# Memory values of block two: computed within the attention and the router of block one instead of among the modulation's loads

## The chip, the cores and the metric

The kernel runs on one core of a Trainium2 chip. The metric is the device time of one execution in microseconds (us), the median of several runs. Engines are named as in the profile: PE is the matrix engine (PEld its weight loads), DVE, ACT and POOL the vector, scalar and general engines, SP the engine that issues most transfers.

## What is computed

Two blocks, one after the other, on 256 tokens of width 1024, all in 32-bit floats. Cut to what matters:

```python
# block one (x, ctx, c)
sh1, sc1, g1, sh2, sc2, g2 = split(silu(c) @ w_mod + b_mod, 6)     # modulation rows; the same for ctx
hx, hc = modulate(rmsnorm(x), sh1, sc1), modulate(rmsnorm(ctx), csh1, csc1)
...                                   # latents (w_in), MLA with 8 heads, neighbourhood attention with 8 heads
x = x + g1 * (concat([o_mla, o_na]) @ w_out)
hx2 = modulate(rmsnorm(x), sh2, sc2)
x = x + g2 * hierarchical_moe(hx2)    # 16 experts of 1024 x 512, router picks one group, two of its experts
# block two (the result of block one, and mem, 256 rows of width 1024)
kv = mem_n @ w_mem_kv                 # mem_n = rmsnorm(mem); 1024 x 2048
k, v = split(kv, 2)                   # "memory keys" and "memory values"
...                                   # w_in_2, convolution, stick-breaking attention
o = memory_cross_attention(q, rmsnorm(k), v)
...                                   # output projections, a feed-forward layer of 4096
```

Memory keys and values depend on `mem` and `w_mem_kv` alone. They may be computed at any time before block two's cross attention. The kernel computes both early and writes them to the scratch tensors `mkd` and `mvd` in device memory, from where block two reads them.

## The kernel before, in words

**Products.** A weight matrix comes in pieces of 128 x 4 x 512 floats (1024 KB, `raw` tiles). Each half of a piece (two groups of 128 rows) is made into a `split` tile: a rounded high part (ACT, L197, every fourth one DVE, L195) and the remainder (DVE, L198). PE then adds up three products: high times high, low times high, high times low (L223). A `Stream` S holds a list of such halves of all its jobs; `S.step()` does the next one, which with two halves of 128 tokens and 512 columns is 12 matmuls of 512 columns. `la[0]` says how many halves ahead the splits are made, `S.hold` where the list stops for now.

**Storage and loads.** The on-chip memory is cut into 24 slots. `take` takes the first of the free slots, `give` returns one. All weight loads stand in one list, `plan`, in a fixed order; `pump` issues the next ones on SP as slots come free (L138). SP works its queue in order: a load whose slot is still being read holds all loads behind it.

**Order of the work.** It is the order in which the program is written; each engine takes its instructions in that order.
1. Modulation (to 68.6 us): the memory keys (2 jobs, `J_mk`, `ev_memk`) and six of the eight steps of the memory values (`J_mv`, `ev_memv`, into the tile `mvt`) are put between the pieces of `w_mod`, whose products (`mod_rows`, L591) need 32 columns of weights only. `memTh`, `memTl` hold the transposed `mem_n`; `ktmp` the keys before their norm, `memk_T` transposes them.
2. `mod_T`: transposes and modulates `x` and `ctx` (ACT writes `md`, L662), and does one S step after each quarter: the last two steps of the values, then `kvl`. After the second quarter it gives `memTh`, `memTl`, and POOL's queue writes `mvt` to `mvd`.
3. Latents and projections of `w_in`; their last job is `nv`.
4. Attention: 32 units (16 neighbourhood units, then 16 MLA units) go through a pipeline of scores (PE L874, L877), maximum (DVE L886, L888), exponential (ACT L889), transposes of P (PE L483), and P times v (PE L912). The generator `latents()` interleaves, with the first half of the units, the MLA queries (`w_uq`) and keys and values (`w_ukv`; ACT L723 writes `kf`, DVE L724 writes `v`).
5. `w_out` (`J_wo`), residual, router (L995 to L1090), `gather` (L1113), which collects the tokens of an expert, then the 16 experts (L1186, L1215), whose weights stream in through `plan`.
6. Block two, whose weights follow in the same list.

Of the kernel before, what the change touches and what calls it, by code (L numbers as in the profile page):

```python
# [86 lines left out]
def body(tc, d, out, dbg=None, stop=None):  # L87
# [80 lines left out]
    class Stream:  # L168
# [62 lines left out]

        def step_w(self, job, s, k, kg, first, last):
# [117 lines left out]
    P_memv = [plan_w(("mv", c), d["w_mem_kv_2"], 1024, 1024 + 512 * c, 512) for c in range(2)]  # L350
    mvq = [plan.pop() for _ in range(4)][::-1]
    plan.append(mvq[0])
    plan_mod(0, range(2, 3))
    plan.append(mvq[1])
    plan_mod(0, range(3, 4))
    plan.append(mvq[2])
    plan_mod(0, range(4, 8))
    plan.append(mvq[3])
# [24 lines left out]
    P_ukv = [plan_w(("ukv", c), d["w_ukv"], 256, 512 * c, 512) for c in range(2)]  # L383
    P_wo = []
    for c in range(2):
        P_wo.append([(("wo", c, h), 4) for h in (1, 0)])
        for h in (1, 0):
            plan.append((("wo", c, h), [128, 4, 512], kpn(d["w_out"][512 * h:512 * h + 512, 512 * c:512 * c + 512])))
    for e in range(NE):
# [147 lines left out]
    mvt = take([128, 2, 1024], F32, "mvt")  # L537

    def ev_memv(c):
        def f(m, ps):  # L540
            A.activation(mvt[:, m, 512 * c:512 * c + 512], ps, AF.Identity, scale=rmem[:, m:m + 1])
# [36 lines left out]
    S.step()  # L578
    memk_T(0)
    sumsq(ss1[:, 0:1], x[:, 0, :])  # L580
    S.step()
    sumsq(ss1[:, 1:2], x[:, 1, :])
    S.step()
# [25 lines left out]
    S.step()  # L609
    next(mr)  # L610
    S.step()
    memk_T(1)
    give(ktmp)
    G.dma_start(mkd, mkT)
    dump("mkT", mkT)
    sumsq(ss1[:, 2:3], ctxt[:, 0, :])
    next(mr)
    S.step()
    sumsq(ss1[:, 3:4], ctxt[:, 1, :])
    S.step()  # L620
# [6 lines left out]
    la[0] = 1  # L627
    S.step()
    la[0] = 0
# [3 lines left out]
    S.ahead(1)  # L633
# [8 lines left out]
    S.ahead(2)  # L642
# [91 lines left out]
    for j in J_uq + J_ukv:  # L734
# [31 lines left out]
    give(mkT, mvt)  # L766
    st["ql"] = take([128, 2, 384], F32, "ql")
    interleave(S.gen(J_ql), (mod_rows(2, range(0, 4)), 1))

# [24 lines left out]
    S.hold = J_ukv[1].end  # L794
# [154 lines left out]
    for j in J_wo:  # L949
        S.add(j)  # L950
    side = latents()
    n = 0
    for i, _ in enumerate(pipeline(32, [at_s0, at_s1, at_s1b, at_s2, at_s3], [0, 0, 1, 3, 4])):
# [55 lines left out]

    S.run(J_wo[1])  # L1010
    give(oTh, oTl, gb[0])
# [28 lines left out]
    keep(1)  # L1040

# [81 lines left out]

    xg[0] = take([128, 8, 256], F32, "xg")
# [667 lines left out]
```

## Time and profile before

| | |
|---|---|
| Median of 3 runs (lowest, highest) | 1113.88 us (1113.6, 1114.24) |
| The profiled execution | 1112.18 us, of which the span of the trace is 1110.4 us |
| PE busy | 1057.2 us, 95% of the span |
| DVE, ACT, POOL busy | 606.0, 434.3, 93.3 us |
| Moved from and to device memory | 254.95 MB, mean 230 GB/s |
| The stages, us from the span's start | modulation to 68.6, latents to 176, attention to 272, `w_out` to 297, router and gather to 318, experts to 562, block two to the end |

A median compares kernels; a row of the trace belongs to the one profiled execution, so sums of rows are set against 1112.18. PE at 95% is a mean over stages: the rows below are cut by stage, since what an added matmul costs depends on whether PE waits there.

### The profile page before, as it was taken

Reading aid. Unit: us, or ns where it says so; the run is one execution under the profiler, and the core shown is the slowest. Engines: PE = TensorE matmul, PEld = TensorE weight load, DVE = VectorE, ACT = ScalarE, POOL = GpSimd, SP = SyncE. Lnnn points to the kernel's source line nnn. Section 1 sums busy time; section 2 is a strip of 40 time slices with the busy share of each in tenths; the row PEclk is TensorE's granted clock in tenths of the full one; section 3 lists DMA queues with packets and bytes.
Section 4 is the critical chain, followed back from the end, with each engine's and each line's share of the span. In section 5 each row is a group of like instructions: output and inputs, shape, how many; then the busy total and the mean of one; then the engine's idle time right before and its main releaser. Section 6 shows DMA issues by size and latency. Waiting matters only on the chain.

```text
span 1110.4 us, 15119 instructions
## 1 busy us (share of the span) xinstructions
PE 1057.2 (95%) x6115; PEld 789.3 (71%) x6115; DVE 606.0 (55%) x930; ACT 434.3 (39%) x744; POOL 93.3 (8%) x99
## 2 busy tenths in 40 slices
PE   5999999899989999998689999999999999999998
PEld 4678876555743434343279878999888889998997
DVE  4554435666534343433175655767455676666544
ACT  4754213556312222222163476444435125343222
POOL 0000303000101010100010444000000000000000
PEclk9999999999989999999899999999999999999999
DMA  9979852454868999999913342534757565545611
GB/s 337 405 259 400 278 181 73 176 190 162 326 230 315 393 395 392 394 395 394 387 61 115 114 153 76 190 124 155 258 184 251 204 207 172 190 154 189 225 41 38
DMA packets 111087, 254.95 MB, mean 230 GB/s; under 512 B 5434, under 2 KB 8475, under 8 KB 108451
## 3 DMA queue, kind: packets, MB, share of 16 engines
q1 hardware_dynamic: 109666, 249.20, 62.4%
q0 software_dynamic: 1344, 4.72, 1.4%
q8 instruction: 50, 0.82, 0.3%
q14 instruction: 27, 0.21, 0.1%
HBM read 249.71 MB, written 4.19 MB: 229 GB/s over the span
## 4 chain that ended last, share of the span: by engine, by line
PE 48%; DMA 1%; DVE 1%; ACT 1%; SPq 0%; issue 0%; DVEq 0%; ACTq 0%
PE acc L223 26%; PE acc L243 11%; PE b L243 7%; DMA raw<-in_w_in 1%; PE b L483 1%; PE b L1499 1%; PE b L1521 1%; PE b L1577 1%; PE b L1601 1%; PE b L1215 0%; PE b L1532 0%; SPq L138 0%; PE b L1520 0%; DVE split L198 0%; ACT junkB L476 0%
## 5 line engine op out<-in xcount | busy, mean ns | idle before, releaser
L198 DVE TENSOR_TENSOR split<-raw,split 128x1024 fp32r<-128x1024 f32 (+2 forms) x226 | 267.5, 1212 | 79.5 <-ACT split L197 77.4
L197 ACT ACTIVATE split<-raw 128x1024 fp32r<-128x1024 f32 (+2 forms) x170 | 168.2, 1035 | 42.4 <-PE acc L223 14.5
L243 PE MATMUL acc<-uh,split 128*128 128x256 f32 x640 | 122.9, 288 | 1.4 <-ACT uh L498 1.4
L1186 PE MATMUL b<-raw,xg 128*64 128x512 f32 x512 | 115.8, 595 | 0.0
L243 PEld LDWEIGHTS acc<-uh,split 128*128 128x128 f32 x640 | 102.7, 193 | 2.5 <-ACT uh L498 1.6
L223 PE MATMUL acc<-split,uh 128*128 128x512 f32 x320 | 101.2, 392 | 0.0
L243 PE MATMUL b<-fh,split 128*128 128x256 f32 x512 | 93.9, 283 | 0.3 <-DVE split L198 0.3
L243 PE MATMUL acc<-ul,split 128*128 128x256 f32 x320 | 91.4, 286 | 0.1
L223 PE MATMUL acc<-split,hidT 128*128 128x512 f32 x384 | 88.4, 389 | 0.0
L223 PEld LDWEIGHTS acc<-split,hidT 128*128 128x128 f32 x384 | 71.6, 188 | 14.6
L243 PEld LDWEIGHTS b<-fh,split 128*128 128x128 f32 x512 | 80.4, 192 | 0.8 <-DVE split L198 0.5
L1186 PEld LDWEIGHTS b<-raw,xg 128*64 128x64 f32 x512 | 36.5, 137 | 61.1 <-issue 59.0
L243 PE MATMUL b<-fl,split 128*128 128x256 f32 x256 | 72.4, 283 | 0.0
L223 PEld LDWEIGHTS acc<-split,uh 128*128 128x128 f32 x320 | 60.1, 188 | 12.8
L1225 ACT ACTIVATE RB<-RA 64x512 fp32r<-64x512 f32 x32 | 20.1, 628 | 121.8 <-DVE RA L1224 120.2
L1215 PE MATMUL b<-raw,RA 128*64 128x512 f32 x256 | 60.0, 611 | 5.3 <-ACT xg L1121 2.5
L243 PEld LDWEIGHTS acc<-ul,split 128*128 128x128 f32 x320 | 61.9, 193 | 0.7 <-DVE ul L499 0.6
L223 PE MATMUL acc<-split,ul 128*128 128x512 f32 x160 | 62.3, 390 | 0.0
L1224 DVE TENSOR_TENSOR RA<-b,gm 64x512 f32<-64x512 f32 x32 | 22.0, 689 | 71.9 <-PE b L1215 71.4
L243 PEld LDWEIGHTS b<-fl,split 128*128 128x128 f32 x256 | 49.1, 192 | 0.3
L1215 PEld LDWEIGHTS b<-raw,RA 128*64 128x64 f32 x256 | 19.0, 141 | 39.8 <-issue 34.4
L223 PE MATMUL acc<-split,memTh 128*128 128x512 f32 x128 | 44.0, 413 | 3.2 <-ACT split L197 1.7
(398 smaller groups left out, 1741.4 us busy)
## 6 DMA issues: line engine op xcount, KB each, us to landing
raw<-in_w_up SPq DMA_DIRECT2D x48, 1024.0 KB, 5.5
raw<-in_w_down SPq DMA_DIRECT2D x48, 1024.0 KB, 9.1
raw<-in_w_in SPq DMA_DIRECT2D x46, 1024.0 KB, 7.9
raw<-in_w_gate SPq DMA_DIRECT2D x32, 1024.0 KB, 14.8
raw<-in_w_mod SPq DMA_DIRECT2D x24, 1024.0 KB, 11.3
raw<-in_w_mem_kv SPq DMA_DIRECT2D x8, 1024.0 KB, 14.1
raw<-in_w_out SPq DMA_DIRECT2D x8, 1024.0 KB, 5.0
raw<-in_w_conv_out SPq DMA_DIRECT2D x4, 1024.0 KB, 4.9
```

The lines of the kernel that those rows point to most:

```text
L197: A.activation(s[:, 0], src, AF.Copy)
L198: V.tensor_tensor(s[:, 1], src, s[:, 0].bitcast(F32), op=OP.subtract)
L223: T.matmul(job.accs[m], x(k + kk), s[:, w, kk, :], start=job.start and first and kk == 0 and j == 0, stop=job.stop and last and kk == kg - ...
L243: T.matmul(bk[:, o:o + 256], s[:, w, kk, 128 * b:128 * b + 128], x(k + kk), start=first and b % per == 0 and r == 0 and kk == 0 and j == 0 ...
L483: T.transpose(bk[0:m, i * 128:i * 128 + p], s, ident)
L1186: T.matmul(b[64 * j:64 * j + 64, :], lt, raw((nm, e, k // 4))[:, k % 4, :], start=(k == 0), stop=(k == 7), skip_group_check=True)
L1215: T.matmul(b[64 * j:64 * j + 64, :], t[:, k, :], raw(("d", e, k // 2))[:, k % 2, 512 * dh:512 * dh + 512], start=(k == 0), stop=(k == 3), ...
L1224: V.tensor_tensor(RA[r, dh, :], b[r, :], gm[r, dh], op=OP.mult)
L1225: A.activation(RB[r, 0, dh, :], RA[r, dh, :], AF.Copy)
L1499: T.matmul(zb[i + j][:, o:o + 256 - k0], skT[sl, p, k0:k0 + 128], sqT[sl, p, k0:256], start=(o == 0), stop=False, skip_group_check=True)
L1521: T.matmul(b[:, 0:384], negL, v, start=False, stop=(n == 1), skip_group_check=True)
L1577: T.matmul(b[:, 0:256], xqT[:, 2 * h + dt, tt * 128:(tt + 1) * 128], mkT[:, 2 * h + dt, :], start=(dt == 0), stop=(dt == 1))
```

## The change

The loads of the memory values leave their places among the `w_mod` pieces. Those of the first job (columns 0 to 511, `J_mv[0]`) stand between `w_ukv` and `w_out`, those of the second behind `w_out`. The matmuls are issued by a new generator, `fine`, which does half a step at a time (6 matmuls of 512 columns, for one half of the tokens): the first job one half-step at every second unit from unit 15 on, that is in the MLA half of the attention; the second job four half-steps in the router, ahead of the matmuls that count the tokens of each expert, and four just ahead of `gather`. `mvt` is taken at unit 15, `memTh` and `memTl` are kept until `gather`, and the write to `mvd` is issued there. The steps that `mod_T` interleaves are then the last two of the memory keys, with their evacuation; `memk_T(1)` and the write of `mkd` move behind `kvl`. While `J_wo[1]` runs, `la[0]` is 4.

```diff
+        def fine(self, job):
+            while self.pos < job.end:
+                i = self.pos
+                while self.nprep <= i:
+                    self.prep(self.nprep)
+                    self.nprep += 1
...
+                for m, (hi, lo) in enumerate(job.lhs):
+                    for kk in range(kg):
+                        for j, (x, w) in enumerate(((hi, 0), (lo, 0), (hi, 1))):
+                            T.matmul(job.accs[m], x(k + kk), s[:, w, kk, :], start=first and kk == 0 and j == 0,
+                                     stop=last and kk == kg - 1 and j == 2)
+                    if last:
+                        job.evac(m, job.accs[m])
+                    if m == len(job.lhs) - 1:
+                        give(s)
+                        pump()
+                        self.pos += 1
+                        if self.nprep <= self.pos < job.end:
+                            self.prep(self.nprep)
+                            self.nprep += 1
+                    yield
...
     plan_mod(0, range(0, 2))
-    P_memv = [plan_w(("mv", c), d["w_mem_kv_2"], 1024, 1024 + 512 * c, 512) for c in range(2)]
-    mvq = [plan.pop() for _ in range(4)][::-1]
-    plan.append(mvq[0])
-    plan_mod(0, range(2, 3))
-    plan.append(mvq[1])
-    plan_mod(0, range(3, 4))
-    plan.append(mvq[2])
-    plan_mod(0, range(4, 8))
-    plan.append(mvq[3])
+    plan_mod(0, range(2, 8))
...
     P_ukv = [plan_w(("ukv", c), d["w_ukv"], 256, 512 * c, 512) for c in range(2)]
+    P_memv = [plan_w(("mv", 0), d["w_mem_kv_2"], 1024, 1024, 512)]
...
+    P_memv.append(plan_w(("mv", 1), d["w_mem_kv_2"], 1024, 1536, 512))
...
-    J_mv = [Job(P_memv[c], 512, mlhs, ev_memv(c)) for c in range(2)]
-    for j in J_mk + J_mv:
+    J_mv = [Job(P_memv[c], 512, mlhs, ev_memv(c), acc=(lambda: [bank(), bank()]) if c else None) for c in range(2)]
+    for j in J_mk:
         S.add(j)
...
     for i, _ in enumerate(mod_T()):
         S.step()
-        if i == 1:
-            give(memTh, memTl)
-            G.dma_start(mvd, mvt)
...
     S.run(J_kvl)
-    give(mkT, mvt)
+    memk_T(1)
+    give(ktmp)
+    G.dma_start(mkd, mkT)
...
-    for j in J_uq + J_ukv:
+    for j in J_uq + J_ukv + J_mv[:1]:
         S.add(j)
...
-    S.hold = J_ukv[1].end
+    S.hold = J_mv[0].end
...
-        elif side:
-            for _ in side:
+        elif mvg is None:
+            for _ in side or ():
                 pass
-            side = None
             lim[:] = [99, 3]
+            mvs["t"] = take([128, 2, 1024], F32, "mvt")
+            mvg = S.fine(J_mv[0])
+        if i >= 15 and i % 2:
+            next(mvg, None)
...
+    la[0] = 4
     S.run(J_wo[1])
+    la[0] = 2
...
     start_y(0, 1)
     keep(1)
+    mvg = S.fine(J_mv[1])
+    for _ in range(4):
+        next(mvg)
...
+    for _ in mvg:
+        pass
+    G.dma_start(mvd, mvs["t"])
+    give(memTh, memTl, mvs["t"])
     xg[0] = take([128, 8, 256], F32, "xg")
     for _ in gather(0):
         pass
```

Three places show what moves on the engines. Lines of the changed kernel have higher numbers: its split is still L197, the evacuations `P` and `kf` are L895 and L728, the matmuls of `fine` L246.

ACT at the start of the attention, before; `P` is the exponential of a unit, `q` and `kf` are evacuations of `w_uq` and `w_ukv` products, `raw_1597` is the second piece of `w_ukv`:

```order
L889 ACTIVATE P_160_1522,sm<-b_1528,sm 128x512
L197 ACTIVATE split_1580<-raw_1515 128x1024
L197 ACTIVATE split_1599<-raw_1597 128x1024
L714 ACTIVATE q_1534<-acc_1583,rq_r 128x384
L714 ACTIVATE q_1534<-acc_1584,rq_r 128x384
L889 ACTIVATE P_160_1522,sm<-b_1624,sm 128x512
L723 ACTIVATE kf_179_1634<-acc_1639,rkv_r 128x4x64
L723 ACTIVATE kf_179_1634<-acc_1640,rkv_r 128x4x64
```

The same place after the change; `raw_1459` is the second piece of `w_ukv`, `raw_1499` the first piece of the memory values:

```order
L895 ACTIVATE P_141_1380,sm<-b_1386,sm 128x512
L197 ACTIVATE split_1442<-raw_1440 128x1024
L197 ACTIVATE split_1461<-raw_1459 128x1024
L719 ACTIVATE q_1392<-acc_1445,rq_r 128x384
L719 ACTIVATE q_1392<-acc_1446,rq_r 128x384
L895 ACTIVATE P_141_1380,sm<-b_1484,sm 128x512
L197 ACTIVATE split_1501<-raw_1499 128x1024
L728 ACTIVATE kf_161_1494<-acc_1504,rkv_r 128x4x64
L728 ACTIVATE kf_161_1494<-acc_1505,rkv_r 128x4x64
```

The split of the first piece of the memory values now stands in ACT's queue between an exponential and the `kf` evacuations.

PE in the MLA half after the change (before, these rows are the same without the L246 ones, with L877 for L883 and L483 for L504); `kT`, `qT` are keys and queries of a pair of heads:

```order
L883 MATMUL b_1897<-kT_169_1551,qT_1617 128x512
L504 MATMUL b_1903<-cst,P_141_1380 128x128 x4
L246 MATMUL acc_1878<-split_1501,memTh_116 128x512
L246 MATMUL acc_1878<-split_1501,memTl_117 128x512
L246 MATMUL acc_1878<-split_1501,memTh_116 128x512 x2
L246 MATMUL acc_1878<-split_1501,memTl_117 128x512
L246 MATMUL acc_1878<-split_1501,memTh_116 128x512
L883 MATMUL b_1919<-kT_169_1551,qT_1617 128x512
L504 MATMUL b_1925<-cst,P_141_1380 128x128 x4
```

Six matmuls of 512 columns stand between every second pair of units.

PE in the router, before; L1008 starts a sum of the output, L1062 to L1064 count tokens, L1113 is `gather`:

```order
L1008 MATMUL acc_2538<-raw_84,cst 128x512
L1008 MATMUL acc_2551<-raw_84,cst 128x512
L1062 MATMUL b_2553<-selm,cst 128x32
L1063 MATMUL b_2553<-selm,ones 128x16
L1064 MATMUL b_2553<-selm,ones 128x32
L1113 MATMUL b_2581<-D_2560,xh_2527 128x256 x2
```

The same place after the change (L1079 to L1081 count tokens):

```order
L1020 MATMUL acc_2514<-raw_84,cst 128x512
L1079 MATMUL b_2516<-selm,cst 128x32
L1080 MATMUL b_2516<-selm,ones 128x16
L1081 MATMUL b_2516<-selm,ones 128x32
L246 MATMUL b_2473<-split_2380,memTh_116 128x512
L246 MATMUL b_2473<-split_2380,memTl_117 128x512
L246 MATMUL b_2473<-split_2380,memTh_116 128x512 x2
L246 MATMUL b_2473<-split_2380,memTl_117 128x512
L246 MATMUL b_2473<-split_2380,memTh_116 128x512
```

24 matmuls of the second job (from `split_2374` and `split_2377`) now stand ahead of the counting, and another 24 (from `split_2380` and `split_2395`) between the counting and `gather`.

## Rows read from the trace of the kernel before

**Rows 1.** Busy by stretch: length, PE, PEld, DVE, ACT, POOL, clock, DMA, GB/s

```profile
13.40:68.50 55.10, 52.64 (x256) 35.88 (x256) 30.07 (x62) 34.34 (x70) 0.72 (x1) 1.00 1.00 380
...
192.00:234.30 42.30, 36.11 (x214) 23.63 (x211) 27.25 (x66) 22.98 (x54) 0.79 (x4) 0.96 0.55 197
234.30:266.00 31.70, 31.70 (x162) 17.53 (x162) 21.66 (x52) 21.79 (x52) 0.00 (x0) 1.00 0.23 81
...
312.00:314.00 2.00, 2.00 (x11) 2.00 (x11) 0.59 (x5) 1.54 (x3) 0.00 (x0) 0.50 0.00 0
320.00:360.00 40.00, 38.06 (x186) 14.03 (x184) 16.43 (x24) 7.98 (x12) 4.86 (x2) 1.00 0.93 332
380.00:400.00 20.00, 20.00 (x101) 7.92 (x97) 5.71 (x10) 3.04 (x5) 0.00 (x0) 1.00 1.04 397
```

**Rows 2.** The chain that ended last: start, length (us), engine, what

```profile
548.22 13.97 DMA raw<-in_w_in
...
1084.42 21.80 PE acc L223 x96
```

**Rows 3.** Timeline of SP's DMA issues: start, length, what

```profile
18.63 0.91 SPq L138 DMA_DIRECT2D raw<-in_w_mod  x2
...
42.02 0.33 SPq L138 DMA_DIRECT2D raw<-in_w_mod  x1
```

**Rows 4.** DMA issues in 18.6:18.7, 42.0:42.1: KB of one, us to landing

```profile
raw<-in_w_mod SPq DMA_DIRECT2D x1, 1024.0 KB, 10.6
...
raw<-in_w_mod SPq DMA_DIRECT2D x1, 1024.0 KB, 12.7
```

**Rows 5.** Timeline of PE, end of the modulation: start, length, line, operation [idle before]

```profile
64.06 3.64 PE L591 MATMUL b<-raw,cond 128*32 128x512 f32 x32
68.57 1.09 PE L483 MATMUL b<-cst,raw 128*128 128x128 f32 x8 [0.87 <-DVE raw L597]
```

**Rows 6.** Timeline of ACT, memory-key and memory-value evacuations

```profile
28.32 0.67 ACT L518 ACTIVATE ktmp<-acc,rmem 128x512 f32<-128x512 f32 x1
...
32.20 0.21 ACT L468 ACTIVATE rk_r<-rk_t 128x4 f32<-128x4 f32 x1
...
75.73 1.50 ACT L541 ACTIVATE mvt<-acc,rmem 128x512 f32<-128x512 f32 x2
```

**Rows 7.** DMA issues in 163.0:163.42 and 182.2:182.6: KB, us to landing

```profile
raw<-in_w_ukv SPq DMA_DIRECT2D x1, 512.0 KB, 4.5
...
raw<-in_w_out SPq DMA_DIRECT2D x1, 1024.0 KB, 5.0
```

**Rows 8.** Timelines at the attention's start: PE, DVE, ACT

```profile
175.24 1.06 PE L591 MATMUL b<-raw,cond 128*32 128x512 f32 x8
...
181.58 0.57 DVE L198 TENSOR_TENSOR split<-raw,split 128x384 fp32r<-128x384 f32 x1
...
189.14 0.83 ACT L723 ACTIVATE kf<-acc,rkv_r 128x256 f32<-128x256 f32 x2
```

**Rows 9.** Timeline of PE, one period of the MLA units

```profile
242.19 1.12 PE L877 MATMUL b<-kT,qT 96*128 96x512 f32 x2
...
247.76 2.41 PE L912 MATMUL acc<-PT,v 128*64 128x256 f32 x16
250.10 1.13 PE L877 MATMUL b<-kT,qT 96*128 96x512 f32 x2
```

**Rows 10.** Timeline of DVE, end of w_out

```profile
295.60 0.69 DVE L941 TENSOR_TENSOR gb<-acc,gb 128x512 f32<-128x512 f32 x1 [5.61 <-PE acc L223]
```

**Rows 11.** Timeline of PE, router and gather

```profile
309.14 0.61 PE L1062 MATMUL b<-selm,cst 128*128 128x32 f32 x2 [4.79 <-DVE selm L1057]
...
311.70 2.05 PE L1113 MATMUL b<-D,xh 128*128 128x256 f32 x8 [1.10 <-DVE tot L1079]
...
318.26 8.80 PE L1186 MATMUL b<-raw,xg 128*64 128x512 f32 x40
```

**Rows 12.** DMA issues in 77.53:77.6: KB, us to landing

```profile
mvd<-mvt POOLq DMA_DIRECT2D x1, 1024.0 KB, 10.0
```

More of the change, by code (lines that the diff above doesn't have):

```diff
@@ L230, in step @@
             self.pos += 1
+        def fine(self, job):
[4 more added lines that the diff above has]
+                    self.nprep += 1
+                job, key, a, k, kg, first, last, done = self.g[i]
+                s = self.prepared.pop(i)
+                if first:
+                    job.accs = job.acc() if job.acc else [bank("acc")[:, :job.n] for _ in job.lhs]
+                for m, (hi, lo) in enumerate(job.lhs):
[13 more added lines that the diff above has]
+                    yield
         def step_w(self, job, s, k, kg, first, last):
@@ L536, in body @@
     mlhs = lhs_of(memTh, memTl, (0, 128))
-    mvt = take([128, 2, 1024], F32, "mvt")
+    mvs = {}
     def ev_memv(c):
         def f(m, ps):
-            A.activation(mvt[:, m, 512 * c:512 * c + 512], ps, AF.Identity, scale=rmem[:, m:m + 1])
+            A.activation(mvs["t"][:, m, 512 * c:512 * c + 512], ps, AF.Identity, scale=rmem[:, m:m + 1])
         return f
     J_mk = [Job(P_memk[c], 512, mlhs, ev_memk(c)) for c in range(2)]
-    J_mv = [Job(P_memv[c], 512, mlhs, ev_memv(c)) for c in range(2)]
-    for j in J_mk + J_mv:
+    J_mv = [Job(P_memv[c], 512, mlhs, ev_memv(c), acc=(lambda: [bank(), bank()]) if c else None) for c in range(2)]
+    for j in J_mk:
         S.add(j)
@@ L577, in body @@
     ss1 = smal([128, 4], "ss1")
-    S.step()
     memk_T(0)
     sumsq(ss1[:, 0:1], x[:, 0, :])
-    S.step()
     sumsq(ss1[:, 1:2], x[:, 1, :])
-    S.step()
     def mod_rows(Tn, ks=range(8)):
@@ L608, in body @@
     next(mr)
-    S.step()
     next(mr)
[L611 to L615, printed above, removed]
     sumsq(ss1[:, 2:3], ctxt[:, 0, :])
     next(mr)
-    S.step()
     sumsq(ss1[:, 3:4], ctxt[:, 1, :])
-    S.step()
     r1 = rstd_of(ss1, 1024, "r1")
@@ L626, in body @@
     next(mr)
-    la[0] = 1
-    S.step()
-    la[0] = 0
     S.step()
@@ L632, in body @@
         pass
-    S.ahead(1)
     mc = mod_cols(0)
@@ L641, in body @@
                                op0=OP.add, op1=OP.mult)
-    S.ahead(2)
     la[0] = 1
@@ L765, in body @@
     S.run(J_kvl)
-    give(mkT, mvt)
+    memk_T(1)
+    give(ktmp)
+    G.dma_start(mkd, mkT)
+    dump("mkT", mkT)
     st["ql"] = take([128, 2, 384], F32, "ql")
     interleave(S.gen(J_ql), (mod_rows(2, range(0, 4)), 1))
+    give(mkT)
     st["kvT"] = take([128, 2, 2, 512], F32R, "kvT")
@@ L948, in body @@
     J_wo = [Job(P_wo[c], 512, wol, ev_wo(c)) for c in range(2)]
-    for j in J_wo:
+    for j in J_wo + J_mv[1:]:
         S.add(j)
     side = latents()
+    mvg = None
     n = 0
@@ L1122, in gather @@
             yield
+    for _ in mvg:
+        pass
+    G.dma_start(mvd, mvs["t"])
+    give(memTh, memTl, mvs["t"])
     xg[0] = take([128, 8, 256], F32, "xg")
```

## The prediction

> **What bounds the kernel now.** I cut the span by stage first: the same 96 matmuls leave one stage and enter three others, and each stage's own limit says what that is worth. In the list of stretches [rows 1] read PE's busy time against the stretch's length, then the granted clock, the DMA share and the GB/s. In the modulation (13.4 to 68.5) PE has 52.64 of 55.10 us and the DMA engines are full at 380 GB/s, so matmuls and loads are both near their limit. In the first half of the attention (192.0 to 234.3) PE has 36.11 of 42.30: it waits for 6.2 us. In the MLA half (234.3 to 266.0) it has 31.70 of 31.70. While the experts run the DMA engines are full, at 397 GB/s in 380 to 400.
>
> Then the chain that ended last, from its end back [rows 2]. It is nearly all PE, down to a load that is issued at 548.22 and lands 13.97 later, at 562.19, after the experts. The 548 us behind that landing hold nothing that the change touches. Ahead of it the experts' loads run at a fixed rate. So the change is worth what it does to the start of the experts, and to those loads.
>
> **The change part by part** (+ is slower).
>
> *1. Modulation: −19.4.* The first `w_mod` load is issued at 18.63 and lands 10.6 later, at 29.2; the last is issued at 42.02 and lands 12.7 later, at 54.7 [rows 3, 4]. Between them land six more of `w_mod` and three of the memory values: ten intervals in 25.5 us, 2.55 each. Without the three, the last lands at 29.2 + 7 × 2.55 = 47.1. Its eight matmuls are a quarter of the group of 32 at 64.06, and then the transposes wait 0.87 for DVE [rows 5]. In the kernel before that wait ends at 68.57; now it would at 47.1 + about 1.1 + 0.9 = 49.1. PE allows it: of the steps in this stage eight are gone (six of the values, and two of the keys that replace values in `mod_T`), 8 × 12 = 96 matmuls. The chain has 96 matmuls of that size in 21.80 us [rows 2], 0.227 each. So PE would be ready at 68.57 − 21.8 = 46.8, before the load's 49.1. I take 49.1; the load's end is the bound now. 68.57 − 49.1 = 19.4.
>
> *2. Key evacuation in `mod_T`: +3.3.* In `mod_T` the values' evacuation, 1.50 us on ACT at 75.73, becomes that of the keys, which runs from 28.32 to 32.41 where the trace has it, 4.1 us with its sums of squares [rows 6]. The next `md` on ACT is 2.6 later, and so are DVE's halves of `hc` and `hx`, the split behind them and the step of `kvl` that waits for it. DVE also gets the norm's own steps; I add 0.7 for these, an estimate. Between 2.6 and 4.1.
>
> *3. `memk_T(1)`: +1.0.* Its eight transposes of 128 x 128 move to a place behind `kvl`, where PE has no gap. Eight of that shape take 1.09 at 68.57 [rows 5].
>
> *4. The load chain at the attention's start: +6.0, and +1.5 for the clock.* In the changed program one slot is handed on three times: the second `w_uq` piece waits for the last reader of `lx`, the end of `nv`, at 175.24 [rows 8]; the second `w_ukv` piece for the split of that; the first piece of the values for the split of `w_ukv`. A load of 512 KB takes 4.5 when the queue is empty, one of 1024 KB 5.0 [rows 7]. In the times of the trace before: `w_uq` lands at 175.2 + 4.5 = 179.7. Its second split ends on DVE at 182.15 (181.58 + 0.57 [rows 8]); `w_ukv` is issued at about 182.7 and lands at 187.2; its two splits on ACT and DVE take some 2.4, the values' piece is issued at 189.6 and lands at 194.6. ACT meets that split ahead of the four `kf` evacuations, as the order shows, and takes 1.1 for it: `kf` starts at 195.7 and not at 189.14 [rows 8]. The units behind it hang on this ACT queue, and PE has nothing in its own queue to put there. 6.5, of which I take 6.0, since the units' chain has some slack. It is 0 if a load lands 6 us sooner, 8 if one is later. An idle PE of that length is followed in this trace by half clock: after 4.79 us of waiting in the router [rows 11] the granted clock is 0.50 [rows 1]. A few us at half clock cost between 0 and 4; I take 1.5.
>
> *5. The first job in the MLA half: +10.9.* 48 matmuls × 0.227. A period of four MLA units runs from 242.19 to 250.10, 7.9 us, with rows back to back [rows 9] and no wait of PE in 31.70 us [rows 1]. The cover would have to be inside PE's own busy rows. Nothing in the stage is later than PE: ACT has 21.79 and DVE 21.66 of 31.70. From both sides: 0 if PE only looks busy, 10.9 if it is. The row of the stage is at the second.
>
> *6. `w_out`: +1.0.* The values' second job wants four splits made ahead (`la` 4). DVE reaches the residual at 295.60 after 5.61 idle [rows 10]; four remainders of about 1.2 each, partly waiting for ACT's high parts, fill that and hang over by 0.6 to 1.
>
> *7. Router and gather: +1.5.* The first 24 matmuls take 5.45 and stand where PE waits 4.79 until 309.14 [rows 11]: +0.7. The second 24 take another 5.45 ahead of `gather`, of which the 1.10 before 311.70 covers part: 4.3 more. Against that PE stays busy there, and `gather`, 6.56 us from 311.70 to 318.26 almost all at half clock [rows 1, 11], should take 3.8 at full clock: −2.8. The 0.7 falls into the same waits for DVE, so I count 4.3 − 2.8.
>
> *8. The experts' loads: +2.0.* `memTh`, `memTl` and `mvt` hold three slots until here, and the load that takes `mvt`'s slot waits on SP for the write to `mvd`, with all loads behind it. That write took 10.0 from issue to landing [rows 12]. There is some cover: in 320 to 360 the loads moved 332 GB/s where 397 can be had [rows 1], 65 × 40 = 2.6 MB, 6.6 us of loading. 10.0 − 6.6 = 3.4, and up to 2.6 more for the write's own 1.05 MB; nothing if the loads issued ahead last. 0 to 6, I take 2.0.
>
> *Sum:* −19.4 + 3.3 + 1.0 + 6.0 + 1.5 + 10.9 + 1.0 + 1.5 + 2.0 = +7.8. Against the profiled execution, 1112.18 (span 1110.4 and 1.8 around it), that is 1120.0. The median of the runs, 1113.88, is 1.7 above that execution, so the median is predicted as 1121.7.
>
> The plain account would be that 96 matmuls are only moved, at no cost, and the loads with them. It isn't so in this trace because they go from a stage that waits for loads afterwards into one where PE has no gap (5), and drag a load into the attention's own chain (4).
>
> **The rivals.**
>
> *B: the load chain doesn't hold ACT (chance 0.18).* The first piece of the values lands before 189, or the NA units run on without `kf`. For it: the first half of the attention leaves PE 6.2 us of waits [rows 1] that could take up lateness. Against it: those waits are the units' own chain. Without term 4 the sum is +0.3: 1114.2.
>
> *C: faster; the first job hides in the MLA half (0.18).* The place is 234.3 to 266.0, the price the 10.9 of term 5, and it decides as soon as more than about 10 us of 31.70 are really free. For it: PEld is busy 17.53 of 31.70 [rows 1], the ends of matmuls in a trace are modelled, and the two score matmuls at 242.19 have 1.12 us where two of 512 columns would take 0.45 at the rate of term 5 [rows 9]. Against it: the sixteen of 256 columns from 247.76 to 250.10 take 0.146 each, near the 0.114 of that rate [rows 9]; the scores multiply plain floats, not the rounded type of the splits, so their length may be real; and no row of PE in the stage names a wait. The sum is −3.1: 1110.8. The Trainium skill, page "Trainium Kernel Development and Optimization", section "Performance Expectations", speaks for this rival: it calls the busy time of matmuls a bad measure of how near a kernel is to its limit, and the share of weight loads a good one. By that rule the MLA half has 45% of PE left, 14 us, and the first job costs nothing. The row with 31.70 of 31.70 says the opposite, and I give it more weight.
>
> *D: slower still (0.12).* The experts' loads starve behind the write (term 8 at 6) and half clock lasts to its bound (4 in term 4): +6.5, 1128.2.
>
> *A: the forecast (0.52):* 1121.7, from 1117 to 1125 with terms 4 and 8 a few us off.
>
> **How the numbers follow.** The likeliest case gives 1121.7. The range goes from 1110.5, which takes in most of C, to 1127.0, which leaves out the most of D. About 0.2%, 2.2 us, is what a measurement of this kernel can tell from no change: faster is below 1111.7, slower above 1116.1. Faster: C, and the few of B in which term 8 or 2 is smaller too, 0.22. Same: most of B, 0.14. Slower: A, D and the rest, 0.64.
>
> **What would show it.** Right: the transposes at 68.57 come near 49; `kvl`'s second step trails by some 3; PE idles 5 to 8 us ahead of the keys' transposes in the first units, with SP issuing the values' load some 5 us before ACT's split; the MLA half is 10 to 11 longer with PE busy throughout; `gather` runs at full clock; the first load after the write to `mvd` is late. Wrong: the MLA half keeps its 31.7 us (C); no wait of ACT for a `raw` tile ahead of `kf` (B); or the modulation ends well after 49, because the loads of `w_mod` find no free slots, which would make the time worse than forecast.

## The result and the profile after

The changed kernel takes 1127.43 us (median of 4 runs, 1123.93 to 1129.18), the kernel before on the same chip 1114.06 (4 runs, 1113.6 to 1114.48): 1.012 times as long, interval 1.0102 to 1.0138. Slower, as forecast, but by 13.4 us where the sum said 7.8; the median is 0.4 above the top of the range (of the four runs, 1123.93 and 1125.83 lie inside it, 1129.04 and 1129.18 above). The profiled executions, 1112.18 and 1125.83, lie 1.9 and 1.6 below these medians and differ by 13.65, so they can be laid side by side. Each stretch ends where a row of PE starts, with three exceptions: the first half of the attention ends, in the kernel after, at the first L246 row, so that all of these matmuls count in the MLA half; the logits end where their PE row ends; block two begins with ACT's first `uh`. Rows of before are in [rows 2, 5, 8, 11].

| stretch of PE | ends before | ends after | change | forecast (term) |
|---|---|---|---|---|
| modulation, to the transposes behind it | 68.57 | 48.62 | −19.95 | −19.4 (1) |
| latents, to the first scores of the attention | 176.23 | 161.46 | +5.18 | +4.3 (2, 3) |
| first half of the attention | 234.27 | 225.61 | +6.11 | +7.5 (4) |
| MLA half, to the first matmul of `w_out` | 272.13 | 276.83 | +13.36 | +10.9 (5) |
| `w_out`, to its last matmul | 296.76 | 301.48 | +0.02 | 0 |
| residual and norm, to the end of the logits | 302.54 | 310.78 | +3.52 | +1.0 (6) |
| router, to `gather` | 311.70 | 325.85 | +5.91 | +4.3 (7) |
| `gather` | 318.26 | 329.67 | −2.74 | −2.8 (7) |
| experts, to the first `uh` of block two | 562.19 | 575.62 | +2.02 | +2.0 (8) |
| the rest | 1112.18 | 1125.83 | +0.22 | 0 |

Windows of the kernel after (columns as in [rows 1]): the modulation, a part of the first half of the attention, the MLA half, the router, `gather`, and a stretch of the experts.

```profile
13.40:48.60 35.20, 30.68 (x152) 18.25 (x152) 20.41 (x45) 22.47 (x46) 0.00 (x0) 0.95 1.01 387
...
182.00:190.00 8.00, 7.12 (x22) 4.20 (x21) 5.19 (x13) 3.08 (x8) 0.00 (x0) 0.50 0.01 2
227.10:270.70 43.60, 40.98 (x204) 25.22 (x203) 23.32 (x53) 24.42 (x55) 0.00 (x0) 1.00 0.35 130
308.00:314.00 6.00, 6.00 (x16) 3.97 (x15) 4.05 (x6) 3.23 (x3) 4.58 (x2) 0.50 0.80 271
...
325.80:329.70 3.90, 3.90 (x35) 3.73 (x34) 1.15 (x3) 1.71 (x3) 0.57 (x1) 1.00 0.98 329
526.00:530.00 4.00, 4.00 (x14) 1.18 (x12) 0.00 (x0) 0.00 (x0) 0.00 (x0) 0.57 1.03 393
```

In the modulation PE now has 30.68 of 35.20 us and the DMA engines are full: the load is the bound, as term 1 had it. The MLA half, which had no gap in [rows 1], now has 2.62 us of them. `gather` has the clock 1.00 that term 7 gave it, but the clock is 0.50 (the 1.2 GHz level) at two places ahead of it, 182 to 190 and 308 to 314, and it falls at two more: 0.50 in 66 to 68, in `mod_T`, and 0.57 in the experts, 526 to 530, where the kernel before had 1.00 at the same work. (The kernel before has one of its own ahead of the router: 0.66 in 228 to 233.)

The waits that the stretches hang on, from the timelines of the kernel after (start, length, engine, line, operation [idle before, and what ended it]); the modulation, `mod_T`, the attention's start, the MLA half, and the end of `w_out` up to the experts:

```profile
46.69 1.07 PE L609 MATMUL b<-raw,cond 128*32 128x512 f32 x8 [0.51 <-DMA raw<-in_w_mod]
48.62 1.09 PE L504 MATMUL b<-cst,raw 128*128 128x128 f32 x8 [0.87 <-DVE raw L615]
...
62.34 0.40 PE L223 MATMUL acc<-split,hc 128*128 128x288 f32 x1 [0.89 <-ACT split L197]
64.71 0.53 PE L223 MATMUL acc<-split,hc 128*128 128x288 f32 x2 [1.84 <-DVE split L198]
...
178.34 1.06 ACT L197 ACTIVATE split<-raw 128x1024 fp32r<-128x1024 f32 x1 [3.15 <-DMA raw<-in_w_mem_kv]
179.91 1.38 PE L504 MATMUL b<-cst,kf 128*96 128x128 f32 x4 [2.69 <-ACT kf L728]
...
243.01 1.22 DVE L198 TENSOR_TENSOR split<-raw,split 128x1024 fp32r<-128x1024 f32 x1 [1.75 <-ACT split L197]
244.16 0.68 DVE L894 TENSOR_REDUCE sm<-b 128x1 f32<-128x512 f32 x1
246.25 1.94 PE L918 MATMUL acc<-PT,v 128*64 128x256 f32 x14 [1.31 <-ACT PT L907]
258.24 1.94 PE L918 MATMUL acc<-PT,v 128*64 128x256 f32 x14 [1.31 <-ACT PT L907]
...
300.09 2.36 DVE L198 TENSOR_TENSOR split<-raw,split 128x1024 fp32r<-128x1024 f32 x2 [1.18 <-ACT split L197]
302.37 0.68 DVE L947 TENSOR_TENSOR gb<-acc,gb 128x512 f32<-128x512 f32 x1
303.84 0.33 PE L504 MATMUL b<-cst,raw 128*128 128x128 f32 x1 [1.33 <-DVE raw L948]
305.16 0.98 PE L504 MATMUL b<-cst,raw 128*128 128x128 f32 x7 [1.00 <-DVE raw L948]
...
311.68 1.42 PE L246 MATMUL b<-split,memTh 128*128 128x512 f32 x1
319.69 0.30 PE L1079 MATMUL b<-selm,cst 128*128 128x32 f32 x2
325.85 1.10 PE L1130 MATMUL b<-D,xh 128*128 128x256 f32 x8
329.67 1.08 PE L1207 MATMUL b<-raw,xg 128*64 128x512 f32 x4
```

Two rows of the kernel before at the same places, `kf`'s transposes and the seven transposes behind the residual:

```profile
191.84 0.67 PE L483 MATMUL b<-cst,kf 128*96 128x128 f32 x4
298.43 0.98 PE L483 MATMUL b<-cst,raw 128*128 128x128 f32 x7 [0.54 <-DVE raw L942]
```

Read each bracket with the row of another engine above it. At 178.34 ACT takes up a split of the memory values that had to wait 3.15 us for its load; `kf` stands behind it, and PE has waited 2.69 when `kf`'s transposes can start. At 243.01 DVE has stood for 1.75 with a remainder (L198) whose high part ACT had not made yet; the maximum of the next unit (L894) stands behind it, and then PE loses 1.31 waiting for a transposed P (PT). At 300.09 two remainders of the second job stand ahead of the residual (L947), and PE waits 1.33 and 1.00 for it. Each time the waiting instruction is at the head of a queue that works in order.

### The profile page after: what moved, and what is told of

Same layout as the page of the kernel before. It is cut to its first block, busy times and chain, and to the rows that moved or that the text cites. A ratio compares the mean times of both kernels' runs of the same rounds, so it can differ in the third digit from the quotient of the medians.

```text
span 1124.0 us, 15124 instructions
## 1 busy us (share of the span) xinstructions
PE 1065.7 (95%) x6115; PEld 792.7 (71%) x6115; DVE 604.2 (54%) x930; ACT 434.9 (39%) x744; POOL 93.0 (8%) x99
## 3 DMA queue, kind: packets, MB, share of 16 engines
q0 software_dynamic: 1344, 4.72, 1.5%
## 4 chain that ended last, share of the span: by engine, by line
PE 49%; DMA 1%; DVE 1%; ACT 1%; issue 0%; SPq 0%; DVEq 0%; ACTq 0%
PE acc L223 25%; PE acc L270 11%; PE b L270 7%; DMA raw<-in_w_in 1%; PE b L504 1%; PE b L1520 1%; PE b L1542 1%; PE b L1598 1%; PE b L1622 1%; PE b L1207 1%; PE b L1236 1%; PE b L1553 0%; PE b L1541 0%; DVE split L198 0%; ACT junkB L497 0%
## 5 line engine op out<-in xcount | busy, mean ns | idle before, releaser
L198 DVE TENSOR_TENSOR split<-raw,split 128x1024 fp32r<-128x1024 f32 (+2 forms) x226 | 267.7, 1212 | 94.7 <-ACT split L197 92.5
L197 ACT ACTIVATE split<-raw 128x1024 fp32r<-128x1024 f32 (+2 forms) x170 | 168.6, 1034 | 63.9 <-PE acc L223 19.3
L270 PEld LDWEIGHTS b<-fl,split 128*128 128x128 f32 x256 | 49.1, 192 | 0.3
L1740 ACT ACTIVATE hid<-b 128x512 f32<-128x512 f32 x16 | 9.5, 595 | 91.3 <-PE b L270 91.3
```

Of the source, the lines that this page charges most:

```text
L197: A.activation(s[:, 0], src, AF.Copy)
L198: V.tensor_tensor(s[:, 1], src, s[:, 0].bitcast(F32), op=OP.subtract)
L270: T.matmul(bk[:, o:o + 256], s[:, w, kk, 128 * b:128 * b + 128], x(k + kk), start=first and b % per == 0 and r == 0 and kk == 0 and j == 0 ...
```

## The experiments

The first four kernels below were compared with a median of before of 1114.26 (9 runs); the one with a third of the second job's matmuls, the two with one job alone and the one with a quarter in the router with 1114.16 (19 runs); the one without the norm and the one with unused matmuls with 1113.73 (17 runs). "Less than after" is against 1127.43. Half clock behind a stretch comes and goes between executions, so each edit is read from the stretch that it touches, and the time stands beside it.

**The splits of the first job later.** From the changed kernel: the list of splits stops ahead of the memory values until unit 15, so that ACT has none of them in the first half of the attention.

```diff
-    S.hold = J_mv[0].end
+    S.hold = J_ukv[1].end
```

> One line changed: the list stops behind w_ukv, so the splits of the memory values' first job are made from unit 15 on and no split waits on ACT ahead of the kf evacuations; the loads keep their order. Theory (term 4 of the forecast, a load holds ACT's queue: kf was 4.95 us later there, relative to the start of the attention, and half clock followed): ACT's kf comes without a wait, the first half of the attention is 4 to 6 us shorter, no half clock at 181 to 191, and the time falls by 3 to 6 us against the changed kernel (1127.4), a little lost again at unit 15 where the first split is now made late. Rival (the units' chain has slack and takes the lateness up by itself): kf comes earlier, the MLA half starts at the same moment, time within 1.5 us of 1127.4.

Measured: 1123.62 (1123.2 to 1124.02), ratio to before 1.008 (1.0058 to 1.0103); 3.8 less than after. ACT's wait for the load is gone, `kf`'s transposes start at 177.24 and not at 179.91, and the granted clock in 181 to 191 is 1.00. PE of this kernel at unit 15:

```profile
222.44 0.50 PE L246 MATMUL acc<-split,memTh 128*128 128x512 f32 x1 [1.42 <-ACT split L197]
...
223.70 0.73 PE L246 MATMUL acc<-split,memTh 128*128 128x512 f32 x2 [0.52 <-DVE split L198]
```

The split has to be waited for here instead. From the first scores to the first L246 it is 60.98 us; 64.15 in the kernel after, 58.04 without the first job. So the chain of term 4 is real: the stretch is 3.2 shorter, 4.6 but for the new wait of 1.42, and rival B falls. Half clock is not gone from the stretch, it comes in 212 to 220. What arrives at the end is less sure than the medians say: in the two traces the lead is 3.2 here, 2.0 at `w_out` and 0.4 at the first expert, and 2.4 at block two, because the stretch at half clock at 525.61 is missing in this execution.

**A third of the first job's matmuls.** From the changed kernel: of each half-step's six matmuls two are issued, for the first job alone (`last_job` is `J_mv[1]`).

```diff
+                            if job is not last_job[0] and (kk, j) not in ((0, 0), (1, 2)):
+                                continue
```

> Only two of every six matmuls of the first job are issued (32 of 48 left out, so its values are not the full products); splits, loads and evacuations stay. Theory (PE is full in the MLA half, term 5): the time falls by 32 x 0.227 = 7.3 us against 1127.4, to about 1120, and the distance from the first MLA unit to w_out shrinks from 51.2 to about 44. Rival C (the matmuls hide there): within 1.5 us of 1127.4, with the same 51 us. A mixture, if the units' softmax is the second bound: 3 to 5 us.

Measured: 1120.53 (1119.92 to 1123.21), ratio 1.0059 (1.0039 to 1.008); 6.9 less than after. The MLA half goes from 51.22 to 45.66. PE of this kernel there:

```profile
242.12 1.94 PE L921 MATMUL acc<-PT,v 128*64 128x256 f32 x14 [2.24 <-ACT PT L910]
```

32 matmuls at 0.227 are 7.3 us; 5.6 come back, since the wait for P, which the matmuls had partly covered, grows from 1.31 to 2.24 at both of its places. Had the job lain in spare time of PE, nothing would have come back. Rival C falls.

**One split in place of four.** From the changed kernel: the first job's splits after the first are left out, and its first split is used for all; all matmuls stay.

```diff
+            if one[0] and job is one[0] and k:
...
+                self.prepared[i] = None
+                return
...
+                if s is None:
+                    s = self.kept
```

> Only the first of the four splits of the first job is made; its matmuls all read that one, so its values are wrong by that, and three times ACT's high part and DVE's remainder are left out of the attention; all matmuls and loads stay. Theory (what the MLA half cost beyond 48 x 0.227: DVE's remainder waits at the head of DVE's queue for ACT's high part, the maximum of the next unit stands behind it, and P times v waits twice 1.31 us for PT): those two waits go, the MLA half is about 2.5 us shorter, time 1125. Rival (the 2.5 us come from PE's own rows, which are longer beside the new matmuls): the waits or the length stay, time within 1 us of 1127.4.

Measured: 1121.32 (1119.59 to 1124.79), ratio 1.0063 (1.0037 to 1.0088). Its profiled execution, 1124.79, lies 3.5 above this median, so only the stretch is read from it: the MLA half takes 48.25 us, 10.4 above the 37.86 of before, and no wait of 1.31 is left. That is the bare price of term 5, and the splits are the other 3.0. The median is 6.1 less than after, where 2.5 had been expected; what the other 3 are isn't shown by this trace.

**Two splits ahead in `w_out`.** From the changed kernel, without `la[0] = 4`.

```diff
-    la[0] = 4
     S.run(J_wo[1])
-    la[0] = 2
```

> The splits ahead during the second w_out job stay at 2 and don't rise to 4. Theory (DVE's two remainders at 300.09 hold the residual by 2.0 us, PE waits 2.3 us there and half clock follows, which also slows the first 24 matmuls of the second job): the residual comes right behind w_out, the logits end about 3 us earlier relative to w_out, and the count of tokens some 3 us earlier; time 1124 to 1125. Rival (the two splits only move into the router, where they hold the comparisons on DVE and the second half of the job waits for them): the gain is given back ahead of gather, time within 1.5 us of 1127.4.

Measured: 1127.46 (1127.06 to 1128.61), ratio 1.0117 (1.0093 to 1.014): no less than after. The stretch to the end of the logits is 5.78 again, as before. DVE and PE of this kernel in the router:

```profile
313.10 1.22 DVE L198 TENSOR_TENSOR split<-raw,split 128x1024 fp32r<-128x1024 f32 x1 [7.11 <-ACT split L197]
...
316.32 0.61 PE L1077 MATMUL b<-selm,cst 128*128 128x32 f32 x2 [3.49 <-DVE selm L1072]
...
324.05 0.50 PE L246 MATMUL b<-split,memTh 128*128 128x512 f32 x1 [1.21 <-ACT split L197]
```

A remainder now blocks the router's comparisons on DVE for 7.11 us, PE waits 3.49 for them and then runs at half clock, and `gather` comes at 329.29 where it came at 325.85. The splits cost PE a wait on either side, as the rival said. In the trace they cost more here: from the last matmul of `w_out` to `gather` it is 29.5 us, 24.4 in the kernel after. The profiled executions differ by only 1.3, since this one has no half clock in `mod_T` (1.5) and a stretch less of it in the experts (1.9 shorter).

**A third of the second job's matmuls.** From the changed kernel, as for the first job.

```diff
+                            if job is last_job[0] and (kk, j) not in ((0, 0), (1, 2)):
+                                continue
```

> Only two of every six matmuls of the second job are issued (16 of 24 left out ahead of the count of tokens, 16 of 24 ahead of gather), so its values are not the full products; splits, loads and evacuations stay. Theory (PE is late for the count: selm stood ready at 315.74 and its matmuls came at 319.69; and the second 24 matmuls stand on the path to gather): from the logits' end to gather 15.1 us become 8 to 10, time 1120 to 1122. Rival (PE idles again in the router, half clock comes back and gather takes 6 us instead of 3.8): 1123 to 1125. If the router's matmuls were hidden: 1127.

Measured: 1118.18 (1116.58 to 1122.91), ratio 1.0048 (1.0028 to 1.0068); 9.2 less than after. From the logits to `gather` it takes 7.43 us and not 15.07: 7.6 less, where 32 matmuls at full clock are 7.3. The experts are 1.2 shorter too. So the matmuls in the router are paid in full. (Of the 9.2 some 1.5 are not theirs: half clock in `mod_T`, which this execution doesn't have. `gather` takes 4.72 here, with a wait of 0.54 for ACT.) PE of this kernel, the counting and `gather`:

```profile
314.39 0.30 PE L1083 MATMUL b<-selm,cst 128*128 128x32 f32 x2
...
316.91 1.10 PE L1134 MATMUL b<-D,xh 128*128 128x256 f32 x8
```

**The second job alone, and the first job alone.** Both from the kernel before, with the generator `fine` and the order of loads for one job; the two pieces of the other job stay among those of `w_mod`, at the first and the last of the four places.

```diff
-    plan_mod(0, range(2, 3))
+    plan_mod(0, range(2, 8))
     plan.append(mvq[1])
...
+    plan.extend(mvq[2:])
...
+    mvg = S.fine(J_mv[1])
+    for _ in range(4):
+        next(mvg)
```

> The kernel before with the second job alone moved, to the router and gather as in the change; the first job stays in the modulation and its half of the values is written there. Theory (each job's 48 matmuls are worth 10.9 us in the modulation, where PE is the bound until the loads take over at 49; the second job costs 3.5 ahead of the logits, 2.3 to the count, 3.6 to gather, less 2.7 in gather): transposes of the modulation at 57 to 58, time 2 to 4 us below the kernel before (1110 to 1112). Rival (the slots held through the attention delay loads, and the experts start short of weights): 1113 to 1116.

```diff
-    plan_mod(0, range(4, 8))
+    plan_mod(0, range(2, 8))
     plan.append(mvq[3])
...
+    plan.extend(mvq[:2])
...
+            mvg = S.fine(J_mv[0])
+        if i >= 15 and i % 2:
+            next(mvg, None)
```

> The kernel before with the first job alone moved, to the MLA half as in the change; the second job stays in the modulation. Theory (10.9 us saved in the modulation; 6.1 lost in the first half of the attention to the load chain and 13.4 in the MLA half): 1121 to 1124. Rival (without the second job behind it the load chain has a free slot, so kf isn't held): 3 to 6 less, 1116 to 1120.

Measured: the second job alone 1111.73 (1110.89 to 1113.28), ratio 0.9979 (0.9968 to 0.9991), 2.4 faster than before; the first alone 1123.64 (1121.9 to 1124.43), ratio 1.0082 (1.0063 to 1.0101), 9.5 slower. Each takes some 10.7 off the modulation (its end at 57.62 and 58.11). The second gives nearly all of it back behind `w_out`: its rows show the waits of 1.43 and 1.00 for the residual and half clock behind them, 10.56 us to the logits. (Its profiled execution, 1112.09, is level with that of before, 1112.18; the 2.4 stands in the medians.) The first gives back more than it got, in the attention: ACT waits 3.16 for the values' load again at 184.09, and the MLA half takes 51.18. PE of the one and ACT of the other:

```profile
289.30 0.33 PE L507 MATMUL b<-cst,raw 128*128 128x128 f32 x1 [1.43 <-DVE raw L962]
290.62 1.75 PE L507 MATMUL b<-cst,raw 128*128 128x128 f32 x7 [1.00 <-DVE raw L962]
```

```profile
184.09 1.06 ACT L197 ACTIVATE split<-raw 128x1024 fp32r<-128x1024 f32 x1 [3.16 <-DMA raw<-in_w_mem_kv]
```

Together they are +7.1, the whole change +13.4. Of the 6.3 between, 5.2 are in one place: the latents' stretch is 0.7 longer with either job alone and 5.18 with both (3.8 more than the two together), since only then do the keys' evacuations fall into `mod_T`, and the modulation gives 19.95 and not 21.4 (1.4).

**Without the norm of the second keys.** From the changed kernel; this shows what term 2 is worth.

```diff
+            if c:
+                return
             for hh in range(2):
```

> The changed kernel without the norm of the second half of the memory keys: ACT still evacuates them in mod_T, but their sums of squares, the inverse root and DVE's scaling are left out, so these keys are wrong. Theory (term 2: what ACT and DVE do for the keys there is on the path to kvl, and half clock follows PE's wait): PE's waits of 0.89 and 1.84 in kvl go and the clock stays up, the attention starts 3 to 4.5 us earlier (157 to 158.5 and not 161.5), time 1123 to 1124.5. Rival (the 5.2 us between the modulation's end and the attention come from the moved transposes and from loads): the attention starts within 1 us of 161.5, time 1127.

Measured: 1123.69 (1123.07 to 1124.27), ratio 1.0092 (1.0074 to 1.011); 3.7 less than after. The attention starts at 157.22 and not at 161.46, 4.24 sooner; of the waits in `mod_T` (0.89 and 1.84 above) one of 0.18 is left. PE of this kernel:

```profile
65.17 0.53 PE L223 MATMUL acc<-split,hc 128*128 128x288 f32 x2 [0.18 <-DVE split L198]
...
157.22 1.13 PE L882 MATMUL b<-nkT,nqT 64*128 64x512 f32 x4
```

So ACT's sums of squares and the norm's steps are on the path, but not all of the 4.24 is theirs. The kernel with two splits ahead in `w_out` has the same program up to here and the same wait of 1.84:

```profile
64.74 0.53 PE L223 MATMUL acc<-split,hc 128*128 128x288 f32 x2 [1.84 <-DVE split L198]
...
159.97 1.13 PE L880 MATMUL b<-nkT,nqT 64*128 64x512 f32 x4
```

Its clock stays at 1.00 behind the wait, and its attention starts 1.5 sooner than that of the kernel after; the two kernels with a third of the matmuls do as it does. So the norm costs 2.8 where the clock stays up, and 1.5 more where it falls, and the same waits are followed by the one or the other.

**A quarter of the values in the router.** From the kernel before: the last 256 of the 1024 columns alone are computed in the router, all of them ahead of the counting; the other 768 stay among the `w_mod` pieces.

```diff
-    P_memv = [plan_w(("mv", c), d["w_mem_kv_2"], 1024, 1024 + 512 * c, 512) for c in range(2)]
+    P_memv = [plan_w(("mv", c), d["w_mem_kv_2"], 1024, 1024 + 512 * c, 512 - 256 * c) for c in range(2)]
...
+    P_memv.append(plan_w(("mv", 2), d["w_mem_kv_2"], 1024, 1792, 256))
...
+    for _ in S.fine(J_mv[2]):
+        pass
```

> The kernel before with a quarter of the values (256 columns, half of the second job, 48 matmuls of 256 columns) moved to the router, all ahead of the count of tokens, none in the attention or ahead of gather. Theory (5.45 us of matmuls leave a stage where PE is the bound, and fit into 4.79 us in which PE waits, which also keeps the clock up for gather): -5.5 in the modulation, +0.7 to the count, -2.7 in gather, 0 to +2 for slots: 1106 to 1110, below both kernels. Rival (the four small splits hold the residual on DVE, and PE's late start makes the count late as in the change): 1111 to 1114.

Measured: 1106.4 (1105.45 to 1107.28), ratio 0.9928 (0.9915 to 0.9942): 7.8 us faster than before and 21 faster than the change. Windows of this kernel: the residual and logits, the counting, and `gather`.

```profile
293.10:298.90 5.80, 5.12 (x30) 3.49 (x29) 4.12 (x12) 3.68 (x10) 0.67 (x1) 1.00 0.80 268
298.90:306.30 7.40, 7.40 (x53) 6.44 (x53) 6.34 (x9) 3.09 (x5) 4.84 (x2) 1.00 0.84 295
308.10:312.00 3.90, 3.85 (x32) 3.80 (x32) 1.97 (x11) 2.75 (x5) 0.00 (x0) 1.00 1.02 390
```

Its 48 matmuls of 256 columns are about 24 of 512, 5.45 us; the wait that they fill is the 4.79 of [rows 11]. The counting is 0.8 later after the logits than before, `gather` runs at clock 1.00 in 3.9 us and not in 6.56, the residual is not harmed (5.78), and the attention starts 3.2 sooner, where 5.5 had been expected of the modulation (it ends 1.9 sooner). At the end of `w_out` the lead is 3.6; the rest comes from `gather`. The experts start at 312.05, 6.2 sooner, and block two at 556.57, 5.6 sooner. (The profiled execution of before lies 2 us under its median here, so the medians are 7.8 apart.)

**Nothing but matmuls in the router.** From the kernel before: 24 matmuls of 512 columns whose result isn't used stand in the router's wait.

```diff
+    fill = bank()
+    for j in range(24):
+        T.matmul(fill, xh[:, 0, 0:128], xh[:, 0, 0:512], start=(j == 0), stop=(j == 23))
```

> The kernel before with 24 matmuls of 512 columns added in the router ahead of the count of tokens; their result is used by nothing, and nothing else is changed. Theory (PE's 4.79 us of waiting there bring half clock into gather; work that fills them costs little and keeps the clock up, which is a part of what the quarter in the router gains): gather 3.8 us instead of 6.6, the count 0.5 to 1.5 later, time 1.0 to 2.5 us below the kernel before although it does 5.45 us more of matmuls. Rival (added matmuls cost their 5.45 us less the 4.79 of waiting and the clock falls all the same): 0.5 to 1.5 us above the kernel before.

Measured: 1112.38 (1111.59 to 1114.83, 12 runs), ratio 0.9994 (0.9984 to 1.0004): no change that can be told, though 5.45 us of matmuls are added. `gather` is at full clock here too (311.27 to 315.17), and the experts start 3.1 us sooner; block two starts at 561.90, 0.3 sooner. PE in the experts, of this kernel and then of the kernel before at the same matmuls:

```profile
511.10 5.35 PE L1218 MATMUL b<-raw,RA 128*64 128x512 f32 x16 [0.52 <-DVE RA L1209]
```

```profile
514.16 3.65 PE L1215 MATMUL b<-raw,RA 128*64 128x512 f32 x16 [0.52 <-DVE RA L1206]
```

The same sixteen matmuls behind the same wait take 1.7 longer; the granted clock in 512 to 516 is 0.57 in the one and 1.00 in the other. The clock's return in `gather` is shown; that it reaches the end is not, in this kernel.

## Why the prediction was right in sign and short in size

The step that failed is the price of the splits in DVE's queue and of the clock behind the waits that they cause. Term 5 put the splits at nothing: the stage is 2.46 longer than its matmuls. Term 6 gave them 1.0 and no clock: 3.52. Term 7 then counted the router's matmuls at full clock: 3.2 and not 1.5.

*1, modulation: held.* 48.62 against 49.1 forecast, with the wait for the last load of `w_mod` as the bound (0.51 at 46.69).

*2 and 3: held, in part by luck.* +5.18 against 4.3. Without the norm 0.9 is left, near the 1.0 of term 3. The norm is 4.3 in this execution, above the 4.1 of my bounds, since 1.5 of half clock follows its waits, which I had not priced; in the three executions without it the two terms together are 3.7.

*4, the load chain: mechanism right, a little too dear.* SP, ACT, `kf` and PE follow each other as forecast, but the values' load is issued at 173.34, sooner than I had it, and ACT waits 3.15 for it: `kf` comes 4.9 later after the attention's start, not 6.5, and PE waits 2.69, not 5 to 8. The half clock behind that wait is longer than I took: of the +6.11, 2.8 are there at `kf`'s transposes (the attention starts 14.8 sooner than before, they come 11.9 sooner, at 179.91 and not at 191.84), and the rest, 3.3, comes after them, in 182 to 190 above all.

*5, the first job in the MLA half: mis-sized by 2.5.* "No row of PE in the stage names a wait" held for the matmuls, which cost their 10.9 (10.4 with one split). The step left out the splits, two of which fall in this half: I had set ACT at 21.79 and DVE at 21.66 of 31.70 [rows 1] and taken them as free. They are free on average, but a remainder that waits for ACT stands in DVE's queue ahead of the next unit's maximum. Two waits of 1.31 are the 2.6. The Trainium skill, page "Trainium Kernel Development and Optimization", section "Performance Expectations", had spoken for rival C by the share of weight loads. The runs don't bear it out here: PEld was at 17.53 of 31.70, and leaving out 32 matmuls shortened this half by 5.6.

*6, `w_out`: mis-sized by 2.5.* The overhang of DVE's remainders was named, as 0.6 to 1. It is two waits, 1.33 and 1.00, where the kernel before has one of 0.54 (before the seven transposes, at 298.43): 1.8 more. The rest is half clock, until 314 (0.50). I had charged half clock in term 4 and not here, though the wait was in my own term.

*7, router and `gather`: mis-sized by 1.7.* The counting comes 2.3 later after the logits than before; I had written 0.7 and counted nothing. That half clock again: the first 24 matmuls take 7.2 (311.68 to 318.84) and not 5.45. The second 24 cost 3.6 against 4.3, and `gather` gives 2.74 against 2.8.

*8, the experts: the size is right by luck, the reason is not.* The write to `mvd` is issued at 327.03, lands 9.0 later, and SP's next load is issued at 336.09: the loads are held, as forecast. But PE doesn't feel it. Its waits in the experts are the same in both kernels, and no load is among them. From the tables of waits, the three longest of the kernel after, PE in 329.7 to 575.6, and of the kernel before, 318 to 562 (engine, line, what it waited for: us, times, longest; L1330 and L1309 are a branch in the program):

```profile
PE b L1181 <- DVEq L1330: 6.3, 1, 6.3
PE b L1225 <- DVE gm L1219: 3.0, 2, 1.5
PE b L1236 <- ACT xg L1138: 2.5, 3, 0.8
```

```profile
PE b L1160 <- DVEq L1309: 6.5, 1, 6.5
PE b L1204 <- DVE gm L1198: 3.0, 2, 1.5
PE b L1215 <- ACT xg L1121: 2.5, 3, 0.8
```

What is longer is a stretch at half clock, where the kernel before has 3.65 at the same place (514.16, above). PE of the kernel after:

```profile
525.61 5.35 PE L1236 MATMUL b<-raw,RA 128*64 128x512 f32 x16 [0.52 <-DVE RA L1227]
```

So the load at the end of the chain [rows 2], on which "the experts' loads run at a fixed rate" rested, was misread. The profile names it as what `uh` waited for, but a small product on DVE (`fgm`) ends just ahead of `uh` too. DVE and ACT of the kernel before, then of the kernel with unused matmuls:

```profile
560.80 1.30 DVE L1432 TENSOR_TENSOR fgm<-cols 128x8 f32<-128x8 f32 x1
562.19 0.47 ACT L498 ACTIVATE uh<-b,fgm 128x256 fp32r<-128x256 f32 x1 [2.53 <-DMA raw<-in_w_in]
```

```profile
560.51 1.30 DVE L1435 TENSOR_TENSOR fgm<-cols 128x8 f32<-128x8 f32 x1
561.90 0.47 ACT L498 ACTIVATE uh<-b,fgm 128x256 fp32r<-128x256 f32 x1 [2.53 <-DVE fgm L1435]
```

In all twelve kernels of this document `uh`, which reads `fgm` and not this load, starts less than 0.1 us behind the end of `fgm`. In the kernel with unused matmuls the load lands at 557.08, 5.1 sooner than before, and block two starts 0.3 sooner.

Terms 5, 6 and 7 are short by 6.6 together, term 4 is 1.4 too large, and all other stretches together are 0.6 above their terms: that is the 5.85 between 7.8 and 13.65. Rival D's number, 1128.2, is near the measured one. Its longer half clock in term 4 came (3.3 and not 1.5), its starved experts didn't: the waits don't show them.

Why the change is slower at all stands in the kernels with one job: the second job alone gains 2.4 and the first alone loses 9.5. PE's full rows in the MLA half were real, so the first job could only be added there. In the router there is one wait of 4.79; a quarter of the values nearly fits it (the counting comes 0.8 later), and a half doesn't (2.1 later with the second job alone).

Open: when half clock comes behind a short wait. In the experts the same matmuls, with the same waits ahead, had 1.00 in one kernel and 0.57 in another, and in `mod_T` the same program had both. I didn't try it further.

## What to carry to other kernels

Move work out of a full stage to where the engine's row shows a wait, and little more of it than that wait holds: 5.45 us of matmuls moved from the modulation into a wait of 4.79 made the kernel 7.8 us faster, 10.9 us at the same place 2.4 faster, and 21.8 us, half of them in a stage without a gap, 13.4 slower. When matmuls are moved, follow what feeds them: each load, split and remainder stands in an in-order queue ahead of something, and it is the position there and not the engine's average load that decides. Price every new wait of PE together with the clock behind it, as a range: here waits of 1.0 to 2.7 us were followed by 6 to 8 us at 0.50, and behind one of 1.84 the clock fell in some executions and not in others. And look at what else ends beside the releaser that a profile names, before a forecast is built on it.

## What the runs showed of the hardware that I had not expected

- Waits of 1.33 and 1.00 us were followed by half clock in 308 to 314; I had expected it behind waits of some 5 us, from [rows 11]. Half clock follows in all six traces that have both waits at this place (1.33 to 1.43, and 1.00), and in none of the five that have one of 0.54 there does it come ahead of the next wait.
- Filling a wait of PE with matmuls, useful or not, gave `gather` its full clock each time (the kernel after, the second job alone, the quarter, the unused matmuls): 3.8 to 3.9 us and not 6.56.
- The runs of one kernel lie in groups about 2 us apart: the 19 runs of before fall into 1112.0 to 1112.3, 1113.4 to 1114.9 and 1116.1 to 1116.3, with a mean granted clock of 0.987 to 0.989, 0.986 to 0.987 and 0.984 to 0.985. One more stretch at half clock costs 1.7 in the experts and 1.5 in `mod_T`, which is near that step; that it is the cause is argued, not shown.
